# Gate products of three quarters by seven products instead of eight, over 1024 columns, in one encoder layer

## The chip, the cores and the metric

The kernel runs on one core of a Trainium2 chip. The metric is the device time of one execution in microseconds (us); less is better. Before the change it is 1462.66 us, the median of three runs (1462.53 to 1464.18).

The engines are called as in the profile: PE is TensorE (matmuls; PEld are its weight loads), DVE is VectorE, ACT is ScalarE, POOL is GpSimd, SP is SyncE, whose queue issues most transfers.

## The reference

One encoder layer for 256 tokens and 2048 features, float32:

```python
h = rms_norm(x, attn_norm)
proj = h @ w_in
qa, ka, va, qb, kb, vb, ga, gb = jnp.split(proj, split_points, axis=-1)   # ga, gb: 2048 columns each
ya = windowed_gqa(qa, ka, va, rel_bias_table, sink_a)
yb = dilated_attention(qb, kb, vb, rel_bias_table)
merged = sigmoid(ga) * (ya @ w_branch_a) + sigmoid(gb) * (yb @ w_branch_b)
x = x + merged @ w_out
hf = rms_norm(x, ffn_norm)
g = dwconv_centred(hf @ w_ffn_gate, conv_w, conv_b)
x = x + (gelu(g) * (hf @ w_ffn_up)) @ w_ffn_down          # 5632 wide
gate_p = sigmoid(rms_norm(x, ple_norm) @ w_ple_gate)
x = x + gate_p * (p @ w_ple_proj)
return rms_norm(x, final_norm)
```

The change touches `h @ w_in` for the columns of the two gates `ga` and `gb`.

## The kernel before, in words

**Blocks and splits.** All weights lie in memory as blocks of 128 x 128, in the order of use, 16 blocks (1 MB) to a piece. SP loads them in halves of 8 blocks into six `raw` buffers. To keep float32 accuracy each half is split: ScalarE copies it to `whi` (rounded, type fp32r), VectorE subtracts to get `wlo` (`split_to`, lines 262 and 263). There are four buffers of each, so the splits can run up to four ahead. The activations are split in the same way into a high and a low part. A product of one 128-row block is then three matmuls: high x high, high x low, low x high.

**The order of the work** is a list of jobs written by `_plan`: keys, queries and values of the attention, then the gates and branches by quarters of 512 columns, then the output projection `o` (two halves of 1024 columns), then the feed-forward layer in two halves (`g` and `u` products of 128 columns each, then `d0` or `d1`, the down projection), then the last gate (`pp`, `pg`). The quarters come in the order

```python
    for quarters in ([0], [1], [2, 3]):
        for c in quarters:
            wide("ga", "w_in", 0, KC, GA, [c])
            wide("gb", "w_in", 0, KC, GB, [c])
        for c in quarters:
            wide("ba", "w_branch_a", 0, QH, 0, [c])
            wide("bb", "w_branch_b", 0, HG, 0, [c])
```

So `ga` and `gb` of a quarter are two jobs of 16 contraction blocks by 512 columns, for two token halves of 128: 16 x 2 x 3 = 96 matmuls of 128 x 512 each (`wide_product`, lines 387 to 389). When one ends, ScalarE applies the tanh straight from the PSUM bank. `ba` (8 blocks, 48 matmuls) and `bb` (4 blocks, 24 matmuls) are the branches; VectorE multiplies them by the gates (lines 917 to 920). A later step, `merge`, transposes the result with eight small matmuls into banks of the tag `pt` and splits it (lines 928, 933, 934); it is hung on a step of the job behind.

**Products by seven.** `o`, `d0` and `d1` are 1024 columns wide and treat two contraction blocks at a time as a 2 x 2 scheme: two token halves by two contraction blocks, times two contraction blocks by two column groups of 512. Eight block products would be needed; in the form of Winograd seven do (`seven_product`, lines 438 to 440), with results p1 to p7 in seven or eight PSUM banks. It needs sums of the activations (`add_up`, split like the rest), and sums of the weights. Not all pairs are done so: `_pairs` gives the order of the pairs of a job and which go by seven. A pair by seven is split in four parts; its first sums of weights come from memory (`back` loads them on the SP queue, line 327), the rest are made by VectorE next to the splits (`t2`, line 271, and `t4`, line 273; for pairs with `_whole` the first of these comes from memory too). `spread_sums` combines the banks p1, p5, p6, p7 after the last pair by seven (lines 875 and 881), while a plain pair that follows keeps TensorE at work.

**Where the sums of weights come from.** `_SEVEN` lists all pairs by seven, 37 of them. The first 14 (`AHEAD`) get their sums in memory by GpSimd's transfers alone (`sums_in_memory`, lines 308 to 315: copies, then accumulating copies), issued during the projections. The others are made during the feed-forward layer: `quarters` loads two tiles on GpSimd's queue, VectorE adds (`sums_of_quarters`, line 296), GpSimd's queue writes them out. That is done every three jobs, 13 times in the first half and 10 times in the second.

**Other names.** `run_due(i, k)` runs what `at` has hung on step k of job i. `x` is the input, feature by feature; its memory is later `res`, the residual, token by token, filled by `fetch`, a quarter at a time, while the gates run. `held["merged"]` holds the split result of the merges, `early` the sums of it for `o`. PSUM has eight banks: tags `acc` (3), `sp` (2), `pt` (2), `misc` (1).

## Time and profile before

| | us |
|---|---|
| median of three runs | 1462.66 |
| the profiled execution | 1463.56 |
| its span (first to last instruction) | 1461.8 |
| PE busy | 1449.2 (99%) |
| PEld busy | 1242.9 (85%) |
| DVE busy | 1086.9 (74%) |
| ACT busy | 819.2 (56%) |
| POOL busy | 123.6 (8%) |
| first quarter, ga, gb, ba, bb | 305.2 to 369.2 |
| second quarter | 369.2 to 429.9 |
| third and fourth quarter | 429.9 to 551.4 |
| output projection, two halves | 551.4 to 636.5 |
| feed-forward first half, g and u | 636.5 to 884.2 |
| d0 | 884.2 to 993.3 |
| feed-forward second half, g and u | 993.3 to 1238.7 |
| d1 | 1238.7 to 1352.3 |

The stages are cut at the first matmul of each. "Busy" joins the durations of the records on an engine; a matmul's record lasts longer than the time until the next one starts, because matmuls are pipelined, so what a matmul costs is read from start to start. The transfers of all queues share 16 DMA engines, and their share is given for stretches of time.

### The profile page before, as it was taken

Reading aid. Unit: us, or ns where it says so; the run is one execution under the profiler, and the core shown is the slowest. Engines: PE = TensorE matmul, PEld = TensorE weight load, DVE = VectorE, ACT = ScalarE, POOL = GpSimd, SP = SyncE. Lnnn points to the kernel's source line nnn. Section 1 sums busy time; section 2 is a strip of 40 time slices with the busy share of each in tenths; the row PEclk is TensorE's granted clock in tenths of the full one; section 3 lists DMA queues with packets and bytes.
Section 4 is the critical chain, followed back from the end, with each engine's and each line's share of the span. In section 5 each row is a group of like instructions: output and inputs, shape, how many; then the busy total and the mean of one; then the engine's idle time right before and its main releaser. Section 6 shows DMA issues by size and latency. Waiting matters only on the chain.

```text
span 1461.8 us, 20555 instructions
## 1 busy us (share of the span) xinstructions
PE 1449.2 (99%) x7531; PEld 1242.9 (85%) x7531; DVE 1086.9 (74%) x1537; ACT 819.2 (56%) x1155; POOL 123.6 (8%) x188
## 2 busy tenths in 40 slices
PE   9999999999999999999999999999999999999997
PEld 8888888888888888888888888888888888888886
DVE  7687665654554468879888888897888876988665
ACT  7465444444444456766555555676555555666653
POOL 0111211100000000201111100102110100010000
PEclk9999999999999999999999999999999999999999
DMA  9798989866656657977888886989888864797652
GB/s 319 258 259 249 258 251 263 256 193 200 204 196 199 211 180 254 297 241 272 269 281 274 281 285 217 286 287 315 273 285 273 298 232 164 254 308 245 215 193 89
DMA packets 114065, 361.11 MB, mean 247 GB/s; under 512 B 12964, under 2 KB 18084, under 8 KB 113836
## 3 DMA queue, kind: packets, MB, share of 16 engines
q1 hardware_dynamic: 88908, 292.80, 59.0%
q0 software_dynamic: 22896, 62.66, 17.1%
q10 hardware_dynamic: 2160, 4.33, 1.0%
q8 instruction: 59, 0.97, 0.3%
q14 instruction: 42, 0.34, 0.1%
HBM read 332.97 MB, written 37.27 MB: 253 GB/s over the span
## 4 chain that ended last, share of the span: by engine, by line
PE 98%; ACT 1%; DMA 0%; DVE 0%; issue 0%; SPq 0%; POOLq 0%; POOL 0%; DVEq 0%; ACTq 0%
PE acc L359 29%; PE acc L362 15%; PE acc L389 9%; PE acc L387 9%; PE acc L388 9%; PE acc L439 7%; PE acc L440 7%; PE acc L438 7%; PE first L336 2%; PE first L337 1%; PE pt L906 1%; PE pt L713 0%; DMA raw<-in_wts 0%; PE sp L672 0%; PE misc L728 0%; PE pt L928 0%
## 5 line engine op out<-in xcount | busy, mean ns | idle before, releaser
L263 DVE TENSOR_TENSOR wlo<-raw,whi 128x1024 fp32r<-128x1024 f32 (+2 forms) x556 | 650.2, 1181 | 219.0 <-ACT whi L262 212.9
L262 ACT ACTIVATE whi<-raw 128x1024 fp32r<-128x1024 f32 (+2 forms) x556 | 562.3, 1022 | 302.4 <-PE acc L389 188.7
L359 PE MATMUL acc<-mov,whi 128*128 128x512 f32 x1840 | 441.6, 391 | 0.0
L359 PEld LDWEIGHTS acc<-mov,whi 128*128 128x128 f32 x1840 | 337.9, 188 | 65.3
L362 PEld LDWEIGHTS acc<-mov,wlo 128*128 128x128 f32 x1840 | 237.3, 191 | 9.1 <-ACT mov L492 0.2
L362 PE MATMUL acc<-mov,wlo 128*128 128x256 f32 x1840 | 242.8, 283 | 0.0
L387 PE MATMUL acc<-whi,mov 128*128 128x512 f32 (+1 forms) x504 | 193.4, 384 | 0.0
L389 PE MATMUL acc<-whi,mov 128*128 128x512 f32 (+1 forms) x504 | 193.1, 383 | 0.0
L388 PE MATMUL acc<-wlo,mov 128*128 128x512 f32 (+1 forms) x504 | 193.0, 383 | 0.0
L476 ACT ACTIVATE t<-acc 128x256 f32<-128x256 f32 x115 | 43.6, 379 | 131.9 <-PE acc L359 131.9
L387 PEld LDWEIGHTS acc<-whi,mov 128*128 128x128 f32 x504 | 95.1, 189 | 18.5 <-DVE first L480 0.5
L389 PEld LDWEIGHTS acc<-whi,mov 128*128 128x128 f32 x504 | 95.1, 189 | 18.4
L388 PEld LDWEIGHTS acc<-wlo,mov 128*128 128x128 f32 x504 | 95.1, 189 | 18.4
L480 DVE TENSOR_TENSOR u<-acc,t 128x256 f32<-128x256 f32 x100 | 42.2, 422 | 71.9 <-ACT t L476 71.0
L865 POOL DMA_DIRECT2D x<-row x36 | 30.9, 870 | 609.4 <-DMA sums<-kept 295.5
L438 PE MATMUL acc<-whi,act 128*128 128x512 f32 x207 | 80.9, 391 | 0.2 <-ACT whi L262 0.2
L439 PE MATMUL acc<-wlo,act 128*128 128x512 f32 x207 | 80.6, 389 | 0.0
L440 PE MATMUL acc<-whi,act 128*128 128x512 f32 x207 | 80.6, 389 | 0.0
L263 DVE TENSOR_TENSOR wlo<-sums,whi 128x1024 fp32r<-128x1024 f32 x37 | 45.1, 1220 | 9.6 <-ACT whi L262 9.5
L817 ACT ACTIVATE c<-c 128x256 f32<-128x256 f32 x44 | 18.3, 417 | 57.6 <-DVE c L816 57.6
L438 PEld LDWEIGHTS acc<-whi,act 128*128 128x128 f32 x207 | 38.8, 188 | 9.1 <-ACT whi L262 1.0
L439 PEld LDWEIGHTS acc<-wlo,act 128*128 128x128 f32 x207 | 38.9, 188 | 8.5
(217 smaller groups left out, 1667.1 us busy)
## 6 DMA issues: line engine op xcount, KB each, us to landing
raw<-in_wts SPq DMA_DIRECT2D x477, 512.0 KB, 5.2
sums<-kept SPq DMA_DIRECT2D x37, 512.0 KB, 5.5
sums<-in_wts POOLq DMA_DIRECT2D x23, 512.0 KB, 7.4
kept<-sums POOLq DMA_DIRECT2D x23, 512.0 KB, 4.4
raw<-in_wts SPq DMA_DIRECT2D x39, 256.0 KB, 5.0
kept<-in_wts POOLq DMA_DIRECT2D x38, 256.0 KB, 8.1
x<-row POOLq DMA_DIRECT2D x36, 256.0 KB, 7.6
kept<-in_wts POOLq DMA_DIRECT2D x14, 512.0 KB, 9.6
```

Source lines behind the costliest of these rows:

```text
L262: nc.scalar.activation(hi, src, AF.Copy)
L263: ins = nc.vector.tensor_tensor(lo, src, hi.bitcast(F32), op=ALU.subtract)
L359: nc.tensor.matmul(acc, hi[:, k, :], m, start=(first and k == 0), stop=(last and k == SUB - 1), skip_group_check=True)
L362: nc.tensor.matmul(acc[:, T:], lo[:, k, :], m[:, :T], start=False, stop=False, skip_group_check=True)
L387: nc.tensor.matmul(acc, xh, hi, start=(k == 0), stop=False)
L388: nc.tensor.matmul(acc, xh, lo, start=False, stop=False)
L389: nc.tensor.matmul(acc, xl, hi, start=False, stop=(k == n - 1 - t * late))
L438: nc.tensor.matmul(acc, xh, hi, start=(e == 1), stop=False)
L439: nc.tensor.matmul(acc, xh, lo, start=False, stop=False)
L440: nc.tensor.matmul(acc, xl, hi, start=False, stop=(e == uses[name]))
L476: keep(nc.scalar.activation(t, acc[:, T:], AF.Copy, scale=scale))
L480: nc.vector.tensor_tensor(u, acc[:, :T], t, op=ALU.add)
```

## The change

In quarters 1, 2 and 3 (not 0) the two jobs `ga` and `gb` become one job `gab`, 1024 columns wide: the first group of 512 columns belongs to `ga`, the second to `gb`. It runs through `seven_product`: of the eight pairs of contraction blocks, taken in the order 0, 4, 1, 2, 6, 3, 5, 7, the pairs 1, 2, 3 and 5 go by seven products.

- The sums of the normed input for these four pairs (`sums_of_input`) are made during `gb` and `ba` of quarter 0, from `x` and the gain, and lie in rows of `held["merged"]` that the late merges fill afterwards.
- The banks p1, p5, p6, p7 are combined by `combined` into the four `th` tiles; at the end each is added to its bank (p2, p3, p4, c22) on VectorE, and ScalarE applies the tanh to the tile.
- Twelve more pairs need sums of weights. `AHEAD` goes from 14 to 20: the twelve of `w_in` (no `_whole`, so three transfers each) and the eight of `w_out` (five transfers each) are made in memory, at jobs listed in `MADE_AT`. The six of `w_ffn_down` that were made in memory before go to the feed-forward layer, 16 and 13 sets, every 2.5 jobs.
- `back` brings the sums of `w_in` into two tiles of the tag `near`, two sets ahead instead of three.
- The PSUM tags of `ba` and `bb` in quarter 1 change (`sp`, `pt`), the merge of quarters 0 and 1 is hung on step 3 of the job behind instead of step 4, and splits of `gab` keep their place in VectorE's order as those of `o`, `d0`, `d1` do.

```diff
+            if c:
+                both = tuple(first + 4 * c + e for first in (GA, GB) for e in range(4))
+                jobs.append(("gab", c, "w_in", both, 0, KC))
+            else:
+                wide("ga", "w_in", 0, KC, GA, [c])
+                wide("gb", "w_in", 0, KC, GB, [c])
...
-AHEAD = 14
+AHEAD = 8 + 3 * 4
+GATED = (1, 2, 3, 5)
+MADE_AT = [*range(11, 34, 2), 34, 35, 36, 37, 38, 40, 42, 45]
...
+    if kind == "gab":
+        return [0, 4, 1, 2, 6, 3, 5, 7], GATED
...
+    if _BLOCKS[a][0] == "w_in":
+        return False
     return _BLOCKS[a][0] == "w_out" or (_BLOCKS[a + SUB][1] % FHALF) // 2 in WHOLE
...
-            if _BLOCKS[a][0] in ("w_out", "w_ffn_down"):
+            if a // PIECE * PIECE in _EIGHT:
                 keep(ins)
...
-                if all(not j <= e < j + 3 for e in _LAST):
+                if all(not j <= e < j + (3 if j > _LAST[0] else 2) for e in _LAST):
                     back()
...
-        t = pairs_of[_SEVEN[j]] = two_sums()
+        t = two_sums() if "ff" in held else ap_.tile([P, SUB, P], F32, name="sums", tag="near", bufs=2)
+        pairs_of[_SEVEN[j]] = t
...
+    def sums_of_input(e):
+        m = GATED[e]
+        two = early_row().rearrange("p (k t) -> p k t", t=T)
+        for k in range(2):
+            nc.scalar.activation(two[:, k, :], x[:, 2 * m + k, :], AF.Copy, scale=gain(0, 2 * m + k))
+        add_up(two, of_input(m))
+
+    def of_input(m):
+        e = SPLIT + 2 * GATED.index(m)
+        return [held["merged"][1][:, e + c, :].rearrange("p (b n) -> p b n", n=P) for c in range(2)]
+
+    def combined(bank, th):
+        (a, c), (b, d) = th["ga"], th["gb"]
+        nc.scalar.activation(a, bank["p1"], AF.Copy)
+        nc.vector.tensor_tensor(b, bank["p6"], a, op=ALU.add)
+        nc.vector.tensor_tensor(c, bank["p7"], b, op=ALU.add)
+        nc.vector.scalar_tensor_tensor(b, bank["p5"], -1.0, b, op0=ALU.mult, op1=ALU.subtract)
+        nc.vector.scalar_tensor_tensor(d, bank["p5"], -1.0, c, op0=ALU.mult, op1=ALU.subtract)
...
-        if FIRST + 4 <= i < FIRST + 4 + 2 * AHEAD and (i - FIRST) % 2 == 0:
-            at((i, 2), sums_in_memory, (i - FIRST - 4) // 2)
+        if i in MADE_AT:
+            at((i, 2), sums_in_memory, MADE_AT.index(i))
+        if kind in ("gb", "ba") and n == 0:
+            for e in range(2):
+                at((i, 3 + 3 * e + 5 * (kind == "gb")), sums_of_input, 2 * (kind == "ba") + e)
+        if kind == "bb" and n == 0:
+            for e in range(2):
+                at((i, 0), back)
+        if kind == "gab":
+            for t in range(2):
+                at((i, 6 + 3 * t), fetch, t, n)
...
-            for e in range(13 if kind == "gg" else len(_SEVEN) - held["asked"]):
-                sums_ahead((i + late + 3 * e, 4), (i + late + 3 * e + 2, 4))
+            for e in range(16 if kind == "gg" else 13):
+                j = i + late + 5 * e // 2
+                sums_ahead((j, 4), (j + 2, 4))
...
-                at((i + 1, 4 if n < QUARTERS - 1 else 2), merge, n, e, held["m"])
+                at((i + 1, (3, 3, 4, 2)[n]), merge, n, e, held["m"])
...
-            tags = {a: b for e in range(2) for a, b in zip(names[e], places[e ^ n])}
+            tags = {a: b for e in range(2) for a, b in zip(names[e], places[e ^ (n != 3 if kind == "gab" else n)])}
...
-            tag = {"pg": ("pt", "acc"), "pp": ("sp", "acc"), "gb": ("sp", "sp"), "ga": ("acc", "acc"), "ba": ("acc", "acc"),
-                   "bb": ("sp", "sp" if n == 1 else "acc")}[kind][n % 2]
+            tag = {"pg": ("pt", "acc"), "pp": ("sp", "acc"), "gb": ("sp", "sp"), "ga": ("acc", "acc"),
+                   "ba": ("acc", "sp" if n == 1 else "acc"), "bb": ("sp", "pt" if n == 1 else "acc")}[kind][n % 2]
...
+        elif kind == "gab":
+            for name, a, t in (("p2", "ga", 0), ("p3", "gb", 0), ("p4", "ga", 1), ("c22", "gb", 1)):
+                u = held["th", n][a][t]
+                nc.vector.tensor_tensor(u, acc[name], u, op=ALU.add)
+                nc.scalar.activation(u, u, AF.Tanh, scale=held["rc"][:, t:t + 1])
```

More of the change, by code (lines that the diff above doesn't have):

```diff
@@ L148, in _stream @@
             order, seven = _pairs(kind, half)
+            _EIGHT.update(range(len(blocks), len(blocks) + KC * len(order), PIECE))
             for m in order:
@@ L159, in _stream @@
     return blocks
-_SEVEN = []
+_SEVEN, _EIGHT = [], set()
 _BLOCKS = _stream()
@@ L1116, in _encoder @@
             acc, _ = wide_product(i, stills["v"], blocks, len(n), "acc", TWINS if far else HALVES)
[L1117 removed]
+        elif kind in ("o", "d0", "d1", "gab"):
             names = ("p2", "p3", "p4", "c22"), ("p1", "p5", "p6", "p7")
             places = ("sp", "sp", "pt", "pt"), ("acc", "acc", "acc", "misc")
[L1120 to L1121 removed]
+            tags = {a: b for e in range(2) for a, b in zip(names[e], places[e ^ (n != 3 if kind == "gab" else n)])}
+            still, sums_at = {"o": (stills["o"], early), "gab": (stills["ga"], of_input)}.get(
+                kind, (lambda k: held["act"][:, k, :], shl))
+            if kind == "gab":
+                if n < QUARTERS - 1:
+                    th = ap_.tile([P, 2, 2, W4], F32, name="th", tag="v", bufs=1)
+                    held["th", n] = {"ga": [th[:, 0, t] for t in range(2)], "gb": [th[:, 1, t] for t in range(2)]}
+                else:
+                    th = ap_.tile([P, 2, W4], F32, name="th", tag="s3", bufs=1)
+                    held["th", n] = {"ga": [th[:, t] for t in range(2)],
+                                     "gb": [ap_.tile([P, W4], F32, name="th", tag="s1", bufs=2) for t in range(2)]}
             end = kind != "d0" and n == 1
             acc = seven_product(i, *_pairs(kind, n), still, lambda m, e: [a[:, e, :] for a in sums_at(m)], tags,
[L1124 removed]
+                                (lambda bank: combined(bank, held["th", n])) if kind == "gab" else
+                                (lambda bank: spread_sums(n, bank, end)))
         elif kind in stills:
[L1126 to L1127 removed]
+            tag = {"pg": ("pt", "acc"), "pp": ("sp", "acc"), "gb": ("sp", "sp"), "ga": ("acc", "acc"),
+                   "ba": ("acc", "sp" if n == 1 else "acc"), "bb": ("sp", "pt" if n == 1 else "acc")}[kind][n % 2]
             acc, rest = wide_product(i, stills[kind], blocks, 4, tag, late=8 if last else 0)
@@ L1142, in _encoder @@
             if kind == "ga":
-                if n < QUARTERS - 1:
-                    th = ap_.tile([P, 2, 2, W4], F32, name="th", tag="v", bufs=1)
-                    held["th", n] = {"ga": [th[:, 0, t] for t in range(2)], "gb": [th[:, 1, t] for t in range(2)]}
-                else:
-                    th = ap_.tile([P, 2, W4], F32, name="th", tag="s3", bufs=1)
-                    held["th", n] = {"ga": [th[:, t] for t in range(2)],
-                                     "gb": [ap_.tile([P, W4], F32, name="th", tag="s1", bufs=2) for t in range(2)]}
+                th = ap_.tile([P, 2, 2, W4], F32, name="th", tag="v", bufs=1)
+                held["th", n] = {"ga": [th[:, 0, t] for t in range(2)], "gb": [th[:, 1, t] for t in range(2)]}
             if kind == "ba":
```

7 lines of the change are left out of this document (1 added, 6 removed).

## The prediction

> **What bounds the kernel now.** I read the busy table first, then the chain that ended last, then the table of stretches, cut at the first matmul of each product.
>
> ```profile
> span 1461.8 us, 20555 instructions
> PE 1449.2 (99%) x7531; PEld 1242.9 (85%) x7531; DVE 1086.9 (74%) x1537; ACT 819.2 (56%) x1155; POOL 123.6 (8%) x188
> PEclk9999999999999999999999999999999999999999
> PE 98%; ACT 1%; DMA 0%; DVE 0%; issue 0%; SPq 0%; POOLq 0%; POOL 0%; DVEq 0%; ACTq 0%
> ```
>
> TensorE is busy 99% of the span, at full granted clock, and is 98% of the chain. A matmul that goes away there should shorten the span by one spacing, unless another engine cannot follow. What a spacing is shows in the second quarter's gb product.
>
> ```profile
> 391.84 0.39 PE L387 MATMUL acc<-whi,mov 128*128 128x512 f32 x1
> 413.37 0.39 PE L389 MATMUL acc<-whi,mov 128*128 128x512 f32 x1
> 391.84:413.60 21.76, 21.76 (x97) 18.02 (x96) 9.81 (x8) 9.74 (x11) 0.00 (x0) 1.00 0.62 204
> 884.23:938.77 54.54, 54.54 (x242) 44.75 (x240) 50.88 (x58) 37.82 (x44) 2.21 (x3) 1.00 0.85 271
> 938.77:993.29 54.52, 54.52 (x241) 44.93 (x240) 49.61 (x55) 37.84 (x44) 5.96 (x8) 1.00 0.89 279
> ```
>
> The columns are stretch, length, then busy time of TensorE, weight load, VectorE, ScalarE and GpSimd, clock, DMA share, GB/s. One record lasts 0.39 us, but 96 matmuls take 21.76 us from first to first: 226.7 ns each. So the record's duration is latency, and 226.7 ns is the price. VectorE is busy only 9.81 of the 21.76 us there, so it has room in this stage. The other two rows are the two halves of the first down projection (d0), which already runs by seven products: 240 matmuls in 54.54 and 54.52 us, 227.2 ns each, with VectorE at 50.88 us. That is how close to the edge such a product runs today.
>
> **TensorE: what goes away.** A pair of contraction blocks over 1024 columns takes 8 products of 3 matmuls; by seven products 21 instead of 24. Three quarters have four such pairs each: 12 x 3 = 36 matmuls of 128x512. 36 x 226.7 ns = 8.16 us. The transposes of the merge, the branch products and everything later keep their counts.
>
> **VectorE in the changed products.** The costs come from these rows.
>
> ```profile
> L263 DVE TENSOR_TENSOR wlo<-raw,whi 128x1024 fp32r<-128x1024 f32 x514 | 624.6, 1223 | 213.0 <-ACT whi L262 206.8
> L263 DVE TENSOR_TENSOR wlo<-raw,whi 128x512 fp32r<-128x512 f32 x39 | 26.7, 686 | 2.9 <-ACT whi L262 2.9
> L273 DVE TENSOR_TENSOR raw<-raw 128x512 f32<-128x512 f32 x37 | 25.3, 685 | 0.0
> L271 DVE TENSOR_TENSOR raw<-raw,sums 128x512 f32<-128x512 f32 x15 | 10.3, 685 | 0.0
> L875 DVE TENSOR_TENSOR row<-acc,row 128x512 f32<-128x512 f32 x12 | 8.2, 687 | 0.2
> L881 DVE SCALAR_TENSOR_TENSOR row<-acc,row 128x512 f32<-128x512 f32 x12 | 7.7, 686 | 0.2
> L262 ACT ACTIVATE whi<-raw 128x1024 fp32r<-128x1024 f32 x514 | 539.5, 1056 | 289.7 <-PE acc L389 188.7 <-PE acc L440 40.5 <-DVE raw L273 23.8
> L262 ACT ACTIVATE whi<-raw 128x512 fp32r<-128x512 f32 x39 | 24.1, 619 | 12.1 <-DMA raw<-in_wts 8.5 <-PE acc L440 3.6
> ```
>
> A plain pair has two splits: 2 x 1.223 = 2.45 us of VectorE against 24 x 0.2267 = 5.44 us of TensorE. A pair by seven products, with both sums of weights made on the spot, has 0.686 + 3 x 1.223 + 2 x 0.685 = 5.73 us against 21 x 0.2267 = 4.76 us: VectorE falls 0.97 us behind in each. A whole product is 4 x 5.73 + 4 x 2.45 = 32.7 us, plus four operations that combine the banks (2.74 us) and four that close them (2.74 us): 38.2 us against 180 x 0.2267 = 40.8 us. ScalarE has 4 x (0.619 + 3 x 1.056) + 8 x 1.056 = 23.6 us plus five copies and tanhs, far from full. So VectorE fits on average at 94%, and the question is the couples of such pairs (1, 2 and 3, 5), where up to 1.9 us of lead must be in stock.
>
> ```profile
> 895.33 3.12 DVE L263 TENSOR_TENSOR wlo<-raw,whi 128x1024 fp32r<-128x1024 f32 x3
> 896.60 0.19 PEld L439 LDWEIGHTS acc<-wlo,shl 128*128 128x128 f32 x1 [0.17 <-DVE wlo L263]
> PE acc L438 <- ACT whi L262: 0.2, 1, 0.2
> ```
>
> In d0 four such pairs come in a row, the first two with both sums on the spot. In the second one the weight load at 896.60 waits 0.17 us for VectorE's split: the stock is just used up after two. Operations back to back also overlap a little (three in 3.12 us, not 3.67), so the real deficit is smaller. The whole loss of d0 is 109.06 - 480 x 0.2267 = 0.24 us for sixteen pairs; for twelve I take 0.2 us.
>
> One thing d0 lacks: in the second and third quarter the merge of the quarter before falls into step 3, right ahead of the first such pair.
>
> ```profile
> 374.61 1.04 PE L928 MATMUL pt<-ident,m 128*128 128x128 f32 x8
> 375.40 0.48 PE L387 MATMUL acc<-whi,mov 128*128 128x512 f32 x1
> 377.05 1.28 DVE L934 SCALAR_TENSOR_TENSOR merged<-pt,merged 128x512 fp32r<-128x512 f32 x2
> ```
>
> Its transposes begin at 374.61 and hold TensorE until 375.40; VectorE has emptied both banks at 378.33, 3.72 us after they began. In the changed product they begin after 36 matmuls (8.16 us), so the `pt` banks are free at 11.9 us; p7 needs the first after 54 matmuls and the transposes, at 54 x 0.2267 + 0.79 = 13.0 us. Margin 1.1 us, about one split in the queue. VectorE's 1.28 us come out of the lead just before it is needed. Bounds: 0 (margin holds) to 2 x 1.28 = 2.6 us; I take 0.3 us, nearer to zero because d0 recovers fully in each plain pair.
>
> **The banks at the end of a product.** p1, p5, p6, p7 are emptied during the last plain pair; the product behind takes the same banks (second to third of the late quarters, and the branch products).
>
> ```profile
> 935.22 1.41 DVE L875 TENSOR_TENSOR row<-acc,row 128x512 f32<-128x512 f32 x2
> 936.66 1.29 DVE L881 SCALAR_TENSOR_TENSOR row<-acc,row 128x512 f32<-128x512 f32 x2
> 938.77 0.39 PE L438 MATMUL acc<-whi,act 128*128 128x512 f32 x1
> ```
>
> d0 does the same four operations, done at 937.95, and the next half, which swaps the same banks, starts on time at 938.77. Queued behind them on VectorE are splits already covered by the plain pair. Cost 0; if the cover went, TensorE would wait up to 2.7 us at three places.
>
> **The new sums of the input** (four sets, each four 128x128 operations and one 128x512, with three ScalarE operations) run beside gb and ba of the first quarter, where VectorE is busy 45% (9.81 of 21.76 us in the like stretch above); they are due only at the second quarter's first such pair. Cost 0. The closing sums and tanhs of a product replace tanhs read from the banks, and have a branch product of 48 matmuls (48 x 0.2267 = 10.9 us) before anyone needs them. Cost 0.
>
> **Queues and loads.** The sums of weights made in memory are a chain on GpSimd's queue that waits for nothing but its own transfers.
>
> ```profile
> 63.47 0.73 POOL L308 DMA_DIRECT2D kept<-in_wts  x1
> 206.53 0.80 POOL L308 DMA_DIRECT2D kept<-in_wts  x1
> 233.31 1.11 POOL L308 DMA_DIRECT2D kept<-in_wts  x1
> 128.00:192.00 64.00, 64.00 (x370) 56.38 (x369) 43.55 (x66) 32.83 (x54) 14.39 (x20) 1.00 0.90 244
> 305.00:369.00 64.00, 64.00 (x302) 53.59 (x301) 33.91 (x37) 28.89 (x34) 0.00 (x0) 1.00 0.60 191
> 363.73:369.17 5.44, 5.44 (x26) 4.51 (x24) 3.65 (x5) 2.12 (x2) 0.00 (x0) 1.00 0.62 197
> 551.43:593.14 41.71, 41.71 (x189) 34.62 (x188) 37.02 (x49) 27.44 (x34) 2.60 (x3) 1.00 0.82 273
> sums<-kept SPq DMA_DIRECT2D x37, 512.0 KB, 5.5
> ```
>
> Eight sets of five transfers take 63.47 to 206.53, 17.9 us each; the two of three transfers that follow 13.4 us each. After: 12 x 13.4 + 8 x 17.9 = 304 us, done near 368 instead of 300. The first twelve are ready at 224, wanted from bb of the first quarter on (363.73); the last eight at 368, wanted from the first output product on (551.43, some 8 us earlier after the change). So from 305 to 368 the DMA share is some 0.90 instead of 0.60, the level at which TensorE stays busy 64.00 of 64.00 us in 128 to 192. Cost 0. On SP the added `back` loads wait for VectorE to read the tile two sets earlier, with raw loads queued behind; from one such read to the next need but one lie at least a pair by seven and a plain pair, over 10 us, against 5.5 us to land. Cost 0.
>
> The Trainium skill, DMA: Bandwidth & Descriptors, section "Issuing engines are not separate DMA queues", says that transfers from all queues interleave on the same 16 engines, so these chains do slow the raw loads. By that rule too the time changes only if the share is full, and the 0.90 row shows room.
>
> **Feed-forward stage.** Six more sets pass through VectorE there (16 and 13 instead of 13 and 10, every 2.5 products instead of 3): 14 more operations.
>
> ```profile
> L296 DVE TENSOR_TENSOR sums<-sums 128x512 f32<-128x512 f32 x23 | 15.7, 684 | 0.0
> 655.00:755.00 100.00, 100.00 (x577) 88.42 (x576) 88.55 (x153) 58.82 (x90) 11.94 (x22) 1.00 0.82 275
> 1000.00:1100.00 100.00, 100.00 (x577) 88.42 (x576) 85.73 (x142) 56.59 (x88) 14.29 (x24) 1.00 0.89 294
> ```
>
> 14 x 0.684 = 9.6 us over two stages of some 230 us, about 2% of VectorE, which has 11% and 14% idle. Cost 0; without that cover, at most the 9.6 us.
>
> **Sum.** -8.16 + 0.2 + 0.3 = -7.66 us. The profiled execution took 1463.56 us (1.76 us around its span), 0.90 us over the median of 1462.66 us; it would become 1455.9 us, the median 1455.0 us.
>
> The Trainium skill, TensorE: Matmul & The Clock Gate, section "Back-to-back issue gap", gives two spacings for 512 columns: 216 ns isolated and about 131 ns sustained. Estimates by them: 36 x 216 = 7.8 us and 36 x 131 = 4.7 us, so 1455.4 or 1458.4 us at the median after the same 0.5 us. The trace's 226.7 ns disagrees with the second.
>
> **Rivals.**
> - *Partial stall.* The couples with the merge run dry, or the banks at three product ends come late: 6 second pairs x 0.97 us = 5.8 us lost, net -2.3 us, 1460.3 us; with half of that 1457.4 us. For it: the 0.17 us wait in d0. Against it: d0 pays 0.24 us for sixteen. Chance 0.11.
> - *The other side: VectorE sets the pace of all twelve.* If no lead is ever rebuilt, each loses its whole 0.97 us: 11.6 us, net +3.5 us, 1466.2 us. It decides from 0.68 us lost per pair (8.16 / 12). Against it: plain pairs leave VectorE 3.0 us each. Chance 0.04.
> - *Loads late*, raw or sums, under the longer chain or the denser stage later: one landing of 5.5 us missed about once, 1460.5 us. Chance 0.04.
> - *The matmuls were cheaper than the mean spacing*: if a removed one frees only its weight load.
>
> ```profile
> L387 PEld LDWEIGHTS acc<-whi,mov 128*128 128x128 f32 x504 | 95.1, 189 | 18.5 <-DVE first L480 0.5
> ```
>
> Then 36 x 0.189 = 6.8 us, less 0.5: 1456.4 us. Against it: the even 226.7 ns. Chance 0.03. The sustained figure of the page above is the sharper form of this one.
>
> **Numbers.** The forecast (stall up to 2.5 us) has 0.78: about 1453.8 to 1457.0 us, the low end being no stall (1454.5) and 0.7 us of spread. About 0.2% (2.9 us, a bound at 1459.7) can be told from no change. Faster: forecast, cheaper matmuls and most of the partial stall, 0.90; same 0.06; slower 0.04. The range reaches into the partial stall: 1453.8 to 1459.0 us.
>
> **What would show it.** TensorE has 36 matmuls fewer and the three products take 41 us each (41.6 with transposes), with weight-load waits on VectorE under 0.5 us in each; VectorE near 94% there; GpSimd's chain ends near 368; later stages keep their lengths, shifted. I am wrong if a product takes over 42.5 us, if TensorE waits for `pt` or `sp` banks, or if TensorE is idle anywhere in the feed-forward stretches.

## The result, and the profile after

The changed kernel takes 1455.42 us (median of four runs, 1455.17 to 1456.24) against 1463.42 us before (four runs, 1462.53 to 1464.58): 8.0 us less, a ratio of 0.9949 with a 95% interval of 0.9936 to 0.9961. The forecast was 1455.0 us with a range of 1453.8 to 1459.0 us.

The profile page after, its span, its busy table and the chain that ended last:

```profile
span 1453.4 us, 20744 instructions
...
PE 1440.8 (99%) x7495; PEld 1236.0 (85%) x7495; DVE 1148.0 (79%) x1643; ACT 843.4 (58%) x1194; POOL 144.8 (10%) x222
...
PE 94%; issue 2%; DMA 2%; ACT 1%; DVE 1%; SPq 0%; POOLq 0%; POOL 0%; DVEq 0%; ACTq 0%
```

TensorE has 7495 instructions instead of 7531, 36 fewer. VectorE works 61 us more and TensorE is still busy 99% of the span. The chain has 94% on TensorE instead of 98%: it now leaves TensorE for one long stretch, in the output projection, which comes up below.

The stretches of the trace show where the 8 us came from. First the whole stage from the first matmul of quarter 1 to the first of the output projection, in the kernel before:

```profile
369.17:551.43 182.26, 182.26 (x818) 151.17 (x816) 96.83 (x100) 82.83 (x88) 0.00 (x0) 1.00 0.60 195
```

Then after: the same stage, the three gate products in it (the first two with the eight transposes of a merge), the second half of the output projection, and a stretch of each half of the feed-forward layer:

```profile
368.72:542.86 174.14, 174.14 (x781) 144.30 (x780) 145.13 (x173) 101.83 (x115) 0.00 (x0) 1.00 0.69 221
368.72:410.43 41.71, 41.71 (x189) 34.61 (x188) 36.33 (x43) 24.85 (x28) 0.00 (x0) 1.00 0.72 227
426.80:468.51 41.71, 41.71 (x189) 34.61 (x188) 36.25 (x42) 24.20 (x27) 0.00 (x0) 1.00 0.71 229
468.51:509.31 40.80, 40.80 (x181) 33.78 (x180) 35.60 (x42) 26.33 (x30) 0.00 (x0) 1.00 0.69 213
584.58:628.02 43.44, 43.24 (x197) 35.17 (x196) 36.41 (x44) 30.01 (x43) 7.11 (x9) 1.00 1.02 316
646.00:746.00 100.00, 100.00 (x577) 88.43 (x576) 88.93 (x153) 58.86 (x90) 12.98 (x24) 1.00 0.84 285
991.00:1091.00 100.00, 100.00 (x577) 88.43 (x576) 87.26 (x144) 57.21 (x88) 15.32 (x26) 1.00 0.91 303
```

The stage went from 182.26 to 174.14 us, which is 8.12 us; whole runs gained 8.0 us by their medians. So the gain lies in this stage, and no loss elsewhere stands out from the spread of whole runs. The third product takes 40.80 us for 180 matmuls, 226.7 ns each, which is the plain spacing. TensorE is busy through all of every product. The feed-forward stretches are still full (100.00 of 100.00 us), with VectorE at 88.93 and 87.26 us there.

The length of this stage is the measure in what follows. In a second set of runs of the changed kernel it came out within 0.01 us (after_again, below), while medians of whole runs differ by about 1 us between chips.

### The profile page after: what moved, and what is told of

It reads as the page before. It is cut to its first block, busy times and chain, and to the rows that moved or that the text cites. A ratio compares the mean times of both kernels' runs of the same rounds, so it can differ in the third digit from the quotient of the medians.

```text
span 1453.4 us, 20744 instructions
## 1 busy us (share of the span) xinstructions
PE 1440.8 (99%) x7495; PEld 1236.0 (85%) x7495; DVE 1148.0 (79%) x1643; ACT 843.4 (58%) x1194; POOL 144.8 (10%) x222
## 4 chain that ended last, share of the span: by engine, by line
PE 94%; issue 2%; DMA 2%; ACT 1%; DVE 1%; SPq 0%; POOLq 0%; POOL 0%; DVEq 0%; ACTq 0%
PE acc L371 29%; PE acc L374 15%; PE acc L451 8%; PE acc L452 8%; PE acc L450 8%; PE acc L401 6%; PE acc L399 6%; PE acc L400 6%; PE first L348 2%; DMA raw<-in_wts 1%; PE first L349 1%; DMA x<-row 1%; PE pt L939 1%; PE pt L725 0%; ACT whi L273 0%
## 5 line engine op out<-in xcount | busy, mean ns | idle before, releaser
L399 PE MATMUL acc<-whi,mov 128*128 128x512 f32 (+1 forms) x312 | 118.5, 380 | 0.0
L401 PE MATMUL acc<-whi,mov 128*128 128x512 f32 (+1 forms) x312 | 118.4, 379 | 0.0
L400 PE MATMUL acc<-wlo,mov 128*128 128x512 f32 (+1 forms) x312 | 118.3, 379 | 0.0
L274 DVE TENSOR_TENSOR wlo<-sums,whi 128x1024 fp32r<-128x1024 f32 x49 | 59.8, 1220 | 11.5 <-ACT whi L273 11.5
L399 PEld LDWEIGHTS acc<-whi,mov 128*128 128x128 f32 x312 | 59.1, 189 | 11.3 <-DVE first L492 0.5
L401 PEld LDWEIGHTS acc<-whi,mov 128*128 128x128 f32 x312 | 59.0, 189 | 10.9
L400 PEld LDWEIGHTS acc<-wlo,mov 128*128 128x128 f32 x312 | 59.0, 189 | 10.9
L273 ACT ACTIVATE whi<-sums 128x1024 fp32r<-128x1024 f32 x49 | 51.8, 1057 | 15.4 <-PE acc L452 8.4
L450 PE MATMUL acc<-whi,merged 128*128 128x512 f32 x136 | 53.1, 391 | 0.0
L451 PE MATMUL acc<-wlo,merged 128*128 128x512 f32 x136 | 53.0, 390 | 0.0
```

Source lines behind the costliest of these rows:

```text
L273: nc.scalar.activation(hi, src, AF.Copy)
L274: ins = nc.vector.tensor_tensor(lo, src, hi.bitcast(F32), op=ALU.subtract)
L399: nc.tensor.matmul(acc, xh, hi, start=(k == 0), stop=False)
L400: nc.tensor.matmul(acc, xh, lo, start=False, stop=False)
L401: nc.tensor.matmul(acc, xl, hi, start=False, stop=(k == n - 1 - t * late))
L450: nc.tensor.matmul(acc, xh, hi, start=(e == 1), stop=False)
```

## The experiments

The theory: the gain is the 36 matmuls at 226.7 ns, whole, because two covers hold: VectorE's splits have enough lead in couples of pairs, and the other work that was moved (banks, merges, sums in memory) hides under full TensorE stretches. The rival: VectorE or a moved piece costs something in the products as well, so more pairs by seven, other orders or other places would change little, or something other than the removed matmuls made the difference. Each kernel below is the changed kernel with the edit shown. "Stage" is the length from the first matmul of quarter 1 to the first of the output projection in its profiled execution; before 182.26, after 174.14 us. Each group of runs has its own runs of the kernel before, on the same chip.

| edit | us | before | ratio (95%) | stage |
|---|---|---|---|---|
| after | 1455.42 | 1463.42 | 0.9949 (0.9936 to 0.9961) | 174.14 |
| after_again | 1456.12 | 1463.22 | 0.9952 (0.9939 to 0.9964) | 174.13 |
| two | 1460.69 | 1464.15 | 0.9975 (0.9965 to 0.9986) | 178.18 |
| row4 | 1458.25 | 1464.15 | 0.9959 (0.9946 to 0.9973) | 176.61 |
| row4_whole | 1456.91 | 1464.15 | 0.9949 (0.9936 to 0.9961) | 174.72 |
| last7 | 1456.15 | 1464.15 | 0.9944 (0.9932 to 0.9957) | 175.69 |
| merge4 | 1456.37 | 1463.68 | 0.9952 (0.9940 to 0.9964) | 174.92 |
| in_memory | 1456.43 | 1463.68 | 0.9954 (0.9942 to 0.9966) | 176.07 |
| five | 1465.00 | 1463.68 | 1.0004 (0.9994 to 1.0015) | 185.92 |
| six | 1478.26 | 1463.68 | 1.0091 (1.0075 to 1.0107) | 196.90 |
| five_clear | 1453.95 | 1463.22 | 0.9935 (0.9922 to 0.9947) | 172.36 |
| six_clear | 1451.86 | 1463.22 | 0.9921 (0.9907 to 0.9934) | 170.75 |
| six_last | 1455.39 | 1463.09 | 0.9942 (0.9929 to 0.9956) | 173.52 |

### Half of the change: two pairs instead of four

```diff
-AHEAD = 8 + 3 * 4
+AHEAD = 8 + 3 * 2
...
-GATED = (1, 2, 3, 5)
+GATED = (1, 2)
-MADE_AT = [*range(11, 34, 2), 34, 35, 36, 37, 38, 40, 42, 45]
+MADE_AT = [*range(11, 38, 2)]
...
-        if kind in ("gb", "ba") and n == 0:
+        if kind == "gb" and n == 0:
```

> Only the pairs 1 and 2 of each product go by seven (six sets of sums of w_in fewer in memory, none moved in the feed-forward layer). Theory (36 matmuls of 226.7 ns are the gain): 18 matmuls, 4.1 us faster than before, half of the change. Rival (part of the gain comes from the width, the moved merges or the moved sums): clearly more than 4.1 us, up to 8; or less, if the fixed parts of the change cost something that the second couple pays for.

The stretches of this kernel, the stage and the second half of the output projection:

```profile
368.54:546.72 178.18, 178.18 (x799) 147.79 (x798) 128.87 (x149) 92.59 (x103) 0.00 (x0) 1.00 0.64 207
588.43:633.10 44.67, 43.39 (x198) 35.11 (x197) 36.35 (x44) 29.61 (x43) 7.12 (x9) 1.00 1.01 303
```

The stage is 4.08 us shorter than before, and 18 x 0.2267 is 4.08: half the matmuls, half the gain. The whole run gained 3.5 us. The other half microsecond may lie in the second row: in this execution the output projection's second half takes 44.67 us, against 43.31 us before and 43.44 us in the changed kernel. That part was not edited; the last section returns to it.

### Four pairs in a row: does the lead matter?

```diff
-        return [0, 4, 1, 2, 6, 3, 5, 7], GATED
+        return [0, 4, 1, 2, 3, 5, 6, 7], GATED
```

> The pairs 1, 2, 3, 5 stand in a row (order 0, 4, 1, 2, 3, 5, 6, 7); same instructions otherwise. In the changed kernel VectorE's lead over TensorE is 0.83 us in the first such pair of a couple and 0.2 us in the second, so each pair with both sums on the spot costs 0.6 us of lead. Theory (a removed matmul pays 226.7 ns only as long as that lead lasts): the third and fourth pair of a row lose 0.4 and 0.6 us, 1.0 us per product, 3 us in all: about 5 us faster than the kernel before instead of 8.0. Rival (VectorE fits on average, the order does not matter): 8.0 us faster, as the change.

The waits of this kernel from 368.90 to 512 us, one line of them (who waited for whom: us, times, longest), and its first product among the stretches:

```profile
PEld acc L451 <- DVE wlo L274: 3.0, 9, 0.5
```

```profile
368.90:411.45 42.55, 42.49 (x190) 34.30 (x188) 38.17 (x45) 25.05 (x28) 0.00 (x0) 1.00 0.71 233
```

The weight loads of the low parts wait for VectorE's subtraction nine times, 3.0 us in all, and the stage is 2.47 us longer than in the changed kernel, where some 3 us were expected. Each product loses 0.84 us. The same matmuls, the same operations, only their order differs: the plain pair (6) between the couples is where the lead is rebuilt. The theory stands here. To see that it is VectorE's time, and nothing else of the order, the next edit keeps the order and takes one of the two additions per pair off VectorE; GpSimd's chain then has to make two more sums for each pair:

```diff
-        return [0, 4, 1, 2, 6, 3, 5, 7], GATED
+        return [0, 4, 1, 2, 3, 5, 6, 7], GATED
...
-    if _BLOCKS[a][0] == "w_in":
-        return False
-    return _BLOCKS[a][0] == "w_out" or (_BLOCKS[a + SUB][1] % FHALF) // 2 in WHOLE
+    return _BLOCKS[a][0] in ("w_in", "w_out") or (_BLOCKS[a + SUB][1] % FHALF) // 2 in WHOLE
```

> As row4, and the first sum of weights of each such pair (t2, one 128x512 operation of VectorE, 0.685 us) comes from memory, as for the output projection: VectorE about level with TensorE in a pair by seven. Theory (VectorE's lead): no stall, 8.0 to 8.2 us faster than before. Rival (the loss of row4 is from the loads or the banks, not VectorE): the same loss as row4, about 5 us faster, or more loss, as each pair now loads 256 KB more.

Its second product among the stretches, and the last transfer of the chain that makes the sums, in the timeline (start, duration, idle time before it):

```profile
427.63:469.34 41.71, 41.71 (x189) 34.62 (x188) 35.94 (x41) 25.26 (x28) 0.00 (x0) 1.00 0.77 264
```

```profile
411.48 0.81 POOL L324 DMA_DIRECT2D kept<-kept  x1 [6.28 <-DMA kept<-in_wts]
```

The second and third products are back at 41.71 and 40.80 us, without a loss. Only the first loses 0.62 us (42.33 us), and it is the one that runs beside the chain, whose last transfer is now issued at 411.48 us. So VectorE's time was what row4 lacked. That the small cost of the first product comes from the longer chain is read from its place here; the runs on the chain below bear it out.

### A plain pair taken away at the end

```diff
-        return [0, 4, 1, 2, 6, 3, 5, 7], GATED
+        return [0, 4, 1, 2, 6, 7, 3, 5], GATED
```

> Order 0, 4, 1, 2, 6, 7, 3, 5: the product ends on a pair by seven, so no plain pair covers the four operations that empty p1, p5, p6, p7. Theory (that plain pair is the cover): TensorE waits at the start of the next job for p5's bank, four operations of 0.68 us less 0.68 us for the first three matmuls, 2 us, up to 4 us with splits queued ahead; three products, 6 to 12 us lost: between 2 us faster and 4 us slower than before. Rival (the banks come free in time anyway): 8 us faster.

The stretch of the branch product behind the first gate product, and its timeline around the wait:

```profile
410.02:421.63 11.61, 11.20 (x49) 8.93 (x48) 10.71 (x14) 7.08 (x9) 0.00 (x0) 1.00 0.70 255
```

```profile
415.24 0.39 PE L401 MATMUL acc<-whi,yab 128*128 128x512 f32 x1
415.30 0.68 DVE L880 SCALAR_TENSOR_TENSOR th<-acc,th 128x512 f32<-128x512 f32 x1
...
416.04 0.50 PE L399 MATMUL acc<-whi,yab 128*128 128x512 f32 x1 [0.41 <-DVE th L880]
```

The expectation missed: 6 to 12 us were to be lost, 1.55 us were. The bank that the branch product needs is released at 415.98 us, 5.96 us after the product began. But TensorE did not stand still until then: its instruction order, set when the kernel is built, puts the 24 matmuls of the other token half first, and only the 25th waits, from 415.24 + 0.2267 us to 416.04 us, some 0.6 us. The price of this lost cover was too high by a factor of about four to eight; that a cover was lost is right.

### The merge one step later

```diff
-                at((i + 1, (3, 3, 4, 2)[n]), merge, n, e, held["m"])
+                at((i + 1, (4, 4, 4, 2)[n]), merge, n, e, held["m"])
```

> The merges of quarters 0 and 1 hang on step 4 of the job behind, as before the change, instead of step 3. Theory (the pt banks must be free before p7): the transposes begin after 48 matmuls instead of 36, 2.7 us later, and the margin of 1.1 us turns into a wait of some 1.6 us in each of two products: about 5 us faster than before instead of 8.0. Rival (the merge is hidden anyway): 8 us faster.

The timeline of the changed kernel at the merge in its first product, then that of this edit:

```profile
376.88 1.03 PE L961 MATMUL pt<-ident,m 128*128 128x128 f32 x8
...
378.65 1.29 DVE L967 SCALAR_TENSOR_TENSOR merged<-pt,merged 128x512 fp32r<-128x512 f32 x2 [1.38 <-ACT merged L966]
```

```profile
379.62 1.03 PE L961 MATMUL pt<-ident,m 128*128 128x128 f32 x8
...
381.45 1.29 DVE L967 SCALAR_TENSOR_TENSOR merged<-pt,merged 128x512 fp32r<-128x512 f32 x2 [2.03 <-ACT merged L966]
...
382.19 0.19 PEld L450 LDWEIGHTS acc<-whi,merged 128*128 128x128 f32 x1 [0.34 <-DVE merged L967]
```

Both banks are empty 3.06 us after the transposes begin (379.94 - 376.88), and 3.12 us after them in the edit, so 2.80 us later on the clock (382.74). But p7 needs only the first of the two. Each of VectorE's two operations takes 0.69 us, so in the edit the first bank is empty at 382.14 us, and the weight load of p7 that waited for it, 0.34 us, starts at 382.19 us. TensorE came to that load after seven other matmuls of the pair. The stage is 0.78 us longer (174.92 us), 0.39 and 0.41 us in the two products that carry a merge, where some 3 us were expected. Step 3 is the better place, and one step later its margin is just used up.

### The down projection's sums left in memory

The change moved six sets of sums out of the chain in memory into the feed-forward layer. This edit moves them back:

```diff
-AHEAD = 8 + 3 * 4
+AHEAD = 8 + 3 * 4 + 6
...
-MADE_AT = [*range(11, 34, 2), 34, 35, 36, 37, 38, 40, 42, 45]
+MADE_AT = [*range(11, 34, 2), *range(34, 48)]
...
-            for e in range(16 if kind == "gg" else 13):
-                j = i + late + 5 * e // 2
+            for e in range(13 if kind == "gg" else 10):
+                j = i + late + 3 * e
```

> All 26 sets of the first part in memory (12 of w_in, 8 of w_out, 6 of w_ffn_down), 13 and 10 sets every 3 jobs in the feed-forward layer as before. Theory (both places are covered): same as the change, 8.0 us faster than before, within 0.5 us; GpSimd's chain ends near 450 instead of 356. Rival (the move to the feed-forward layer was needed, since loads come late where the DMA share is high): the three products lose over 1 us.

The first gate product and the branch product behind it among its stretches, three of the waits in the branch product, and the end of the chain in the timeline:

```profile
368.07:409.78 41.71, 41.71 (x189) 34.61 (x188) 34.55 (x40) 23.37 (x26) 9.46 (x13) 1.00 0.96 302
409.78:422.63 12.85, 11.18 (x49) 8.93 (x48) 9.46 (x13) 7.73 (x9) 2.19 (x3) 1.00 1.02 326
```

```profile
PEld acc L399 <- DVE th L880: 2.1, 1, 2.1
...
PE acc L399 <- DVE th L880: 1.7, 1, 1.7
...
ACT whi L273 <- DMA raw<-in_wts: 1.6, 2, 0.9
```

```profile
428.92 1.11 POOL L324 DMA_DIRECT2D kept<-in_wts  x1
```

It was expected to make no difference, and cost 1.93 us of the stage. The chain issues its last transfer at 428.92 us. The first gate product runs beside it at a DMA share of 0.96 and still takes 41.71 us, as in the changed kernel; the loss is in the branch product, where the share is 1.02. There ScalarE waits for the halves of the weights (`raw`) 1.6 us, and a late split holds up what is queued behind it on VectorE, among it the operation that frees a bank (L880). TensorE waits 1.7 us for that one. So moving six sets to the feed-forward layer was worth 1.9 us of the stage, though the medians of whole runs (7.25 us faster than before) do not tell the two kernels apart. In the changed kernel the chain ends much earlier, and yet fills the transfers while it runs; its timeline, and a stretch of the first quarter beside it:

```profile
63.00 0.72 POOL L319 DMA_DIRECT2D kept<-in_wts  x1
...
208.29 1.14 POOL L319 DMA_DIRECT2D kept<-in_wts  x1
...
347.38 0.81 POOL L326 DMA_DIRECT2D kept<-kept  x1 [7.16 <-DMA kept<-in_wts]
```

```profile
330.00:352.00 22.00, 22.00 (x99) 18.22 (x98) 10.09 (x9) 9.83 (x11) 2.98 (x4) 1.00 0.99 290
```

At a DMA share of 0.99 TensorE is busy 22.00 of 22.00 us: `ga` and `gb` of the first quarter, by eight products, have their weights in time.

### More pairs by seven: five and six of eight

If the gain is only the number of matmuls, five pairs remove 45 and six 54. VectorE's time is taken care of as in row4_whole. Both also move the merges of quarters 0 and 1 out of the gate products, into the branch products behind them. Left out below (`...`) are the lists of places that grow with the number of pairs.

```diff
-AHEAD = 8 + 3 * 4
+AHEAD = 8 + 3 * 5                  # six: 8 + 3 * 6
...
-GATED = (1, 2, 3, 5)
+GATED = (1, 2, 3, 5, 6)            # six: (1, 2, 3, 5, 6, 7)
...
-        return [0, 4, 1, 2, 6, 3, 5, 7], GATED
+        return [0, 4, 1, 2, 3, 5, 6, 7], GATED      # six: [0, 1, 2, 3, 5, 6, 7, 4]
...
-    if _BLOCKS[a][0] == "w_in":
-        return False
-    return _BLOCKS[a][0] == "w_out" or (_BLOCKS[a + SUB][1] % FHALF) // 2 in WHOLE
+    return _BLOCKS[a][0] in ("w_in", "w_out") or (_BLOCKS[a + SUB][1] % FHALF) // 2 in WHOLE
...
-                at((i + 1, (3, 3, 4, 2)[n]), merge, n, e, held["m"])
+                at((i + (2, 3, 1, 1)[n], (2, 4, 4, 2)[n]), merge, n, e, held["m"])
```

> Five pairs by seven (1, 2, 3, 5, 6 in a row), the first sum of weights from memory, merges of quarters 0 and 1 moved behind the products (steps of ba). 45 matmuls fewer than before. Theory: 45 x 0.2267 = 10.2 us faster than before. Rival (VectorE or the loads are full at four): no faster than the change, 8 us or less.

> Six pairs by seven in a row (1, 2, 3, 5, 6, 7, plain pairs 0 and 4 around them), otherwise as the run with five. 54 matmuls fewer than before. Theory: 54 x 0.2267 = 12.2 us faster than before, if VectorE's lead (about level per pair) and the loads (some 11 MB in 39.4 us, 280 GB/s, with GpSimd's chain beside them) hold. Rival (VectorE at 97 to 100%, or a DMA share of 1.0): 2 us or more of it lost, 10 us faster or less.

Both fell. Five: the branch product and the third gate product among the stretches, the wait in that branch product in the timeline, and the last transfer of its chain:

```profile
410.54:429.07 18.53, 13.44 (x57) 10.76 (x56) 11.99 (x15) 8.84 (x12) 3.61 (x5) 0.91 1.01 312
480.05:520.17 40.12, 40.12 (x178) 33.22 (x177) 36.25 (x40) 28.20 (x32) 0.00 (x0) 1.00 0.79 260
```

```profile
416.92 0.79 PE L397 MATMUL acc<-whi,yab 128*128 128x512 f32 x1 [5.09 <-DVE th L878]
...
469.39 0.81 POOL L324 DMA_DIRECT2D kept<-kept  x1 [6.29 <-DMA kept<-in_wts]
```

Six: its first product among the stretches, where TensorE is busy 43.15 of 46.64 us at a share of 1.02:

```profile
368.49:415.13 46.64, 43.15 (x176) 33.33 (x174) 36.49 (x40) 26.08 (x29) 9.11 (x13) 0.96 1.02 323
```

In five the third product, which begins after the chain's last transfer was issued at 469.39 us, takes 40.12 us: 177 x 0.2267, no loss at all. The two before it take 41.82 and 45.54 us. This pointed to the transfers, but the edits had changed VectorE's load as well. So the next two keep five and six and take the chain away from the sixth (seventh) set on. They leave out the rest of the sums and so do not compute the layer; only their times count:

```diff
+        if j >= 5:                 # six_clear: 6
+            kept[j] = kept[j % 5]
+            return
         src = wts[_SEVEN[j] // PIECE].rearrange("p (b n) -> p b n", n=P)
```

> As the run with five pairs, but GpSimd's chain makes only the five sets of the first product; all later sets of w_in and w_out load these (the sums of the other sets are left out, so the output differs). All loads of the products stay. Theory (five and six lost to transfers: the chain beside the products' own loads): 45 matmuls of 226.7 ns, about 10.2 us faster than before, products of 40.1 us. Rival (VectorE is full): the products stay over 41.5 us, as in the run with five, and the gain is 8 us or less.

> As the run with six pairs, with GpSimd's chain cut to six sets in the same way (the rest of the sums left out). Theory (transfers): 54 matmuls, about 12 us faster than before, products of 39.5 us; a little less if the products' own loads, some 280 GB/s, fill the queues. Rival (VectorE is full with six pairs in a row): products over 42 us, 4 us faster or less.

The changed kernel itself ran again beside these two, unedited, under the name after_again:

> The changed kernel once more, on the same chip as the two runs below and beside the kernel before. 36 matmuls fewer: 8.2 us less in the three products, about 8.0 us faster than before.

The first product of each among the stretches, five_clear and then six_clear:

```profile
367.79:407.91 40.12, 40.12 (x179) 33.22 (x177) 35.05 (x39) 25.04 (x27) 0.00 (x0) 1.00 0.77 270
```

```profile
369.06:408.50 39.44, 39.44 (x175) 32.67 (x174) 37.40 (x42) 26.93 (x29) 0.00 (x0) 1.00 0.82 288
```

With the chain gone every product of five_clear takes 40.12 us, and the first of six_clear 39.44 us, which is 174 x 0.2267. VectorE carries 37.40 of 39.44 us there (95%) without one wait showing as lost time. The second and third product of six_clear lose 0.6 us together; there weight loads wait 1.0 us for VectorE's splits and ScalarE waits 3.0 us for a half of the weights. So it was the transfers that held up five and six, hardly VectorE, and not the moved merges, which stand in both pairs of kernels. Nor were the sums themselves late: while the stage ran, SP's queue waited for the chain's transfers 0.4 us in five and 0.6 us in six. The stage shrinks by 4.08 (18 matmuls), 8.12 (36), 9.90 (45) and 11.51 us (54), against 4.08, 8.16, 10.20 and 12.24 us by count.

### Six pairs where the chain allows it

Last, six pairs in the last product only, with `_whole` there, and four in the others:

```diff
-AHEAD = 8 + 3 * 4
+AHEAD = 8 + 2 * 4 + 6
...
-GATED = (1, 2, 3, 5)
+GATED = (1, 2, 3, 5, 6, 7)
...
-        return [0, 4, 1, 2, 6, 3, 5, 7], GATED
+        return ([0, 1, 2, 3, 5, 6, 7, 4], GATED) if c == 3 else ([0, 4, 1, 2, 6, 3, 5, 7], GATED[:4])
...
-        return False
+        return _BLOCKS[a + SUB][2] % KC >= 12
...
-                at((i + 1, (3, 3, 4, 2)[n]), merge, n, e, held["m"])
+                at((i + (2, 3, 1, 1)[n], (2, 4, 4, 2)[n]), merge, n, e, held["m"])
```

> Six pairs by seven in the last product only (in a row, first sum of weights from memory), four as in the change in the other two; merges of quarters 0 and 1 behind the products. 42 matmuls fewer than before. GpSimd's chain grows by two sets and by two transfers in six of them, to near 400 us, so it runs on through most of the first product. Theory (VectorE's lead and the chain): 42 x 0.2267 = 9.5 us, less 0 to 2 us for late loads while the chain still runs: 7.5 to 9.5 us faster than before; the last product 39.4 to 40.1 us. Rival (six pairs in a row stall whatever the chain does): the last product above 42 us, no faster than the change.

The last product and the second half of the output projection among the stretches of six_last:

```profile
468.28:507.90 39.62, 39.62 (x176) 32.55 (x175) 38.01 (x43) 29.30 (x33) 0.00 (x0) 1.00 0.84 275
584.08:630.14 46.06, 44.20 (x198) 34.75 (x197) 36.44 (x44) 30.27 (x45) 7.12 (x9) 1.00 0.96 294
```

The stage gains 0.62 us more than the change (173.52 us). The last product is 1.18 us shorter, as expected. The first branch product gives back some 0.6 us of that: it takes 12.35 us, against 10.88 us for its 48 matmuls and 0.91 us for the merge that moved into it, and a weight load there waits 0.7 us for VectorE to free a bank (L880). The whole run is 7.7 us faster than before, the change 8.0 and 7.1 us in its two sets of runs: not told apart. The output projection's second half is 2.6 us longer in the profiled execution, the slowest of the five runs (1457.53 us; the median is 1455.39 us), so its row cannot be taken for the typical one. No complete version tried here beats the change measurably.

## Why the prediction was right

**The main term.** 36 matmuls at 226.7 ns were to save 8.16 us. The stage is 8.12 us shorter, 225.6 ns for each, and half the dose gave half. The rival "matmuls cheaper than the spacing" (189 ns each, 6.8 us) is out. So is the sustained figure of the Trainium skill, TensorE: Matmul & The Clock Gate, "Back-to-back issue gap": 36 x 131 ns would be 4.7 us. Its isolated figure of 216 ns is nearer to what each removed matmul gave.

**VectorE in the couples: 0.2 us taken, nothing measured.** The changed kernel's waits in the stage have no line in which TensorE waits for a split. The timeline at the tightest place:

```profile
381.85 1.23 DVE L274 TENSOR_TENSOR wlo<-raw,whi 128x1024 fp32r<-128x1024 f32 x1 [0.78 <-ACT whi L273]
...
383.60 0.69 DVE L282 TENSOR_TENSOR raw<-raw,sums 128x512 f32<-128x512 f32 x1
...
384.20 1.22 DVE L274 TENSOR_TENSOR wlo<-sums,whi 128x1024 fp32r<-128x1024 f32 x1
...
385.33 0.69 DVE L284 TENSOR_TENSOR raw<-raw 128x512 f32<-128x512 f32 x1
...
385.94 1.22 DVE L274 TENSOR_TENSOR wlo<-raw,whi 128x1024 fp32r<-128x1024 f32 x1
...
387.23 1.22 DVE L274 TENSOR_TENSOR wlo<-raw,whi 128x1024 fp32r<-128x1024 f32 x1
...
387.31 0.19 PEld L451 LDWEIGHTS acc<-wlo,merged 128*128 128x128 f32 x1
```

The split that starts at 385.94 ends at 387.16, and the weight load ahead of the matmul that reads it starts at 387.31: the lead is down to 0.15 us, but not out. The step that was mis-sized is the deficit of a pair. It was priced with durations, 5.73 us; from start to start the addition at 383.60 costs 0.60 us, the split at 384.20 1.13 us and the addition at 385.33 0.61 us, because the next operation begins before the last one's record ends.

With 1.13 and 0.61 us a pair takes 3 x 1.13 + 3 x 0.61 = 5.22 us where nothing waits. As it ran, the last splits of the two pairs of the couple start 5.38 us apart (381.85 and 387.23). That is 0.62 us over TensorE's 4.76 us, and not 0.97. The prediction had seen an overlap in d0, but misread its row: the three splits in 3.12 us are two whole ones and one of half the columns, which come to 3.13 us by their durations, so that row shows next to none.

The Trainium skill, Vector Engine (DVE) Microarchitecture Reference, "Measured stream behaviour on trn2", has the price with overlap, measured on integers: 1.0417 ns for a column and about 75 ns for each instruction. The estimate by it is 1.142 us for 1024 columns and 0.608 us for 512. The trace agrees (1.13 and 0.60 to 0.61 us).

With 0.97 us a couple would have used up 1.9 us of lead; with 0.62 us it uses 1.2. row4 fits from the other side: four in a row use up 2.5 us by this price, and each product lost 0.84 us, so some 1.6 us of lead had been in stock.

**The merge ahead of the couple: 0.3 us taken, nothing measured.** The prediction let p7 wait until both banks were empty, 3.72 us after the transposes begin. p7 needs only the first, which is empty 2.46 us after them in the changed kernel (378.65 + 0.69 - 376.88), so the margin was some 2.4 us rather than 1.1. merge4, 2.74 us later, used it up and lost 0.39 and 0.41 us.

**The banks at the end of a product.** The zero was right, the cover named for it (the plain pair) only in part. The bound of 2.7 us at three places was too high: with the plain pair gone, last7 lost 0.73, 0.50 and 0.37 us, since the other token half's matmuls come first.

**The chain on GpSimd's queue.** Its end was put near 368 us with nothing lost. It issues its last transfer at 347.38 us and so ends about 7 us later, near 354 us: twelve sets took 145.3 us (208.29 - 63.00), 12.1 us each and not 13.4. The zero was right. The share was to be 0.90 and goes to 0.99 (1.00 from 305 to 330 us), and TensorE still loses nothing beside it; that time is lost only when the share is full, as the prediction said, fits these runs. Products by seven ran beside the chain without loss at 0.96 in in_memory. At 1.00 the first product of row4_whole lost 0.62 us, and at 1.02 the first products of five and six lost 1.7 and 7.2 us (41.82 against 40.12, 46.64 against 39.44 us). What the prediction did not see is how near the edge the kernel stands: six sets more in the chain cost 1.9 us (in_memory), and the full chains of five and six cost 13.6 us (185.92 - 172.36) and 26.2 us (196.90 - 170.75) of the stage. These two figures come from one execution each; five ran from 1461.0 to 1469.2 us, and by medians against before the two chains cost some 11 and 26 us. The prediction's rival "loads late" had the right mechanism; in the changed kernel the chain ends some 15 us before the first product begins. The Trainium skill, DMA: Bandwidth & Descriptors, "Issuing engines are not separate DMA queues", says that the transfers of all queues interleave on the same 16 engines; the rows at shares of 1.01 and 1.02, with weights arriving late, agree. It names no share from which time is lost; that step was the prediction's own.

**What was costed at nothing** was nothing: the feed-forward stretches are full, the sums of the input run beside the first quarter (VectorE 10.09 of 22.00 us in the stretch shown), and the branch products behind the gates cost no more than 0.05 us extra (one weight load waits 0.2 us). VectorE was to be near 94% in the products and is at 87% (35.60 of 40.80 us), again the overlap.

The sum was -7.66 us, the stage gave -8.12 us, and the median is 0.4 us above the forecast; these half microseconds are inside the spread of whole runs. That the median came so close is in part luck: the 0.5 us of stall was not there, and the kernel before ran 0.8 us slower in this set of runs than in the one the forecast started from (1463.42 against 1462.66 us), so two errors partly cancel.

## What to carry to other kernels

When TensorE is full at 99%, price a removed matmul by the spacing from start to start, and price the engine that must keep up with it by start to start as well, not by the durations of its records, which overlap. Then ask of each piece of moved work when it ends and what will run beside it: transfers that cost nothing at a DMA share of 0.96 or 0.99 cost up to 26 us in kernels where it reached 1.02. What a lost cover costs depends on what else TensorE may do first, so read the order of its instructions before naming a price.

## What the runs showed of the hardware that was not expected

A wait on TensorE can cost more than itself. In five the wait of 5.09 us is followed by a matmul record of 0.79 us instead of 0.39 (row at 416.92), and the granted clock over that branch product is 0.91, where the 1.7 us wait of in_memory left it at 1.00. A stretch of that branch product shows the clock itself:

```profile
416.50:419.91 3.41, 2.99 (x7) 2.37 (x8) 3.41 (x6) 1.34 (x2) 0.00 (x0) 0.50 1.03 395
```

For 3.41 us the clock is 0.50, which costs about half of that time, 1.7 us, by estimate. In six four such stretches, 20.5 us together, are at 0.50 or 0.51, so up to some 10 of the 26.2 us there are the clock's. The Trainium skill, TensorE: Matmul & The Clock Gate, "What's actually happening", has it that the clock falls to half after one idle window of some 3.4 us and needs as long to come back; the rows agree.

The second half of the output projection took 46.06 us in the profiled execution of six_last, 44.67 us in that of two, and from 43.07 to 43.93 us in all others, although no edit touched it. It runs at a DMA share of about 1, and its end waits for transfers, as the chain of the changed kernel shows:

```profile
549.39 29.60 issue
579.00 7.88 DMA x<-row
592.92 9.23 DMA raw<-in_wts
```

This is where that chain leaves TensorE. The transposes at the end of the projection need `x`, which accumulating transfers from `row` fill. That these transfers cause the whole spread was not tried; it is one place where whole runs differ while the edited stage does not. Medians therefore could not order edits that differ by about 1 us (last7 gained 8.0 us as a whole and 6.6 us in its stage), and the stage lengths were used.
